# Modulation columns in tiles and on a DMA queue of their own, and the scratch of the expert selection in the free end of a ring buffer

## The chip, the core and the metric

The kernel runs on one core of one Trainium2 chip. The metric is the device time of the whole kernel in microseconds (us). A core has five engines that run beside each other and wait for one another through semaphores: TensorE (PE: matrix products; PEld are its weight loads), VectorE (DVE), ScalarE (ACT), GpSimd (POOL) and SyncE (SP), which here only issues transfers from HBM.

## The reference

Two layers work on 256 tokens of width 1024. Each layer has a token mixer (layer 0 a gated short convolution, layer 1 differential attention) and then a PEER block; each of these four sub-layers is modulated by `shift`, `scale` and `gate` and closed by a layer norm:

```
m = silu(c) @ ada_w + ada_b ;  shift, scale, gate = split(m, 3)
h = x * (1 + scale) + shift
x = layer_norm(ALPHA * x + (1 + gate) * f(h)) * ln_g + ln_b
```

PEER scores 2 x 128 keys for each of 8 heads, takes the best 16 on either side, the best 16 of their pairs (g, the softmax of those), and then sums `g * gelu(h . u[idx]) * v[idx]` over the chosen experts. There are 128 x 128 experts, and u and v are 16384 x 1024 each.

## The kernel before

PEER is computed densely: for all experts, with a gate matrix that is zero where an expert is not chosen. The 128 blocks of 128 experts are taken in three parts, `CHUNKS = (0, 46, 88, 128)`. A *U step* (24 products of 256 columns) forms the activations of a block, which go through gelu into `ring`, a buffer of 88 blocks. A *G step* forms the gates of eight tokens for all blocks of a part (one-hot matrices A and B on VectorE, 16 small products on TensorE) and multiplies them into the ring (line 840). A *V step* (12 products of 512 columns, line 874) adds a block's part to the output in four accumulators. The order is: U of part 0 beside the selection of the experts; U of part 1 with G of part 0; V of part 0 mixed with U of part 2 and G of part 1; V of the rest of parts 0 and 1 with G of part 2; then V of part 2 alone, 40 steps, called the last third of V here (it is 480 of 1536 products). The place between the last G step and V of part 2 is called the junction: V of part 2 can't start before every gate of part 2 is in the ring.

Every matrix weight comes as a 128 x 1024 tile (512 KB) into a pool `raw` and is split in two: ScalarE copies the high part (`spt<-raw`, line 87), VectorE subtracts it to get the low part (`spt<-raw,spt`, line 90). The V steps split their activations in the same way (`wh`, `wl`), once for two steps. TensorE multiplies high by high, high by low and low by high. `raw` has STREAM = 6 tiles (12 more in the convolution, 4 more in attention), `spt` has SPBUFS = 10. `pipeline(steps, 3)` starts the loads and splits of a step three steps before its products.

The modulation is computed by columns on VectorE: a column is 128 outputs of `silu(c) @ ada_w`, one 512 KB load and one multiply-and-sum of 128 x 1024 (line 177); eight make a unit, and a short addition puts a unit into `mod`. There are 96 columns. Those of the first sub-layer and some more are done in the convolution; 48 are spread over the PEER block of layer 0 and eight over that of layer 1, by a generator `fill` that `steps` advances: two columns a call, issued on SP's queue into the same `raw` tiles as the weights:

```
w = raw()
sync.dma_start(w, ada_w[i, s, part, n])
return lambda: dve.scalar_tensor_tensor(w, w, 1.0, csb, op0=ALU.mult, op1=ALU.mult, accum_out=dst)
```

`late` (`Norm.affine`, line 297) multiplies X by ln_g and adds ln_b of the norm before, from two more `raw` tiles; `prep` (line 196) transposes the gate into rows.

The program fixes what each engine computes, but a scheduler of the framework sets the order on each engine, from its own estimate of the times. `behind(name)` and `issue_after` tell it that an instruction must not be put ahead of a named one; an instruction on an engine waits in that order, so that one which waits holds up all behind it on its engine.

Of the kernel before, what the change touches and what calls it, by code (L numbers as in the profile page):

```python
# [11 lines left out]
F32 = mybir.dt.float32  # L12
F32R = mybir.dt.float32r
F16 = mybir.dt.float16
# [22 lines left out]
CHUNKS = (0, 46, 88, 128)  # L37
SPBUFS = 10
STREAM = 6
RING = CHUNKS[2]  # L40
# [3 lines left out]
def tile_trunk(ctx: ExitStack, tc: tile.TileContext, x, c, columns, ada_w, ln_g, ln_b, conv_w_in_a, conv_w_in_b,  # L44
# [134 lines left out]
    def ada_unit(i, s, part):  # L179
# [7 lines left out]
        yield  # L187

    def mod_rows(i, s, part, pool):

        t = pool.tile([P, D], F32, tag="a", name="rows")
        for hf in range(2):
            ps = bank()
            for q in range(4):
                n = 8 * part + 4 * hf + q
                pe.transpose(ps[:, q * P:(q + 1) * P], mod[:, 2 * i + s, n:n + 1].to_broadcast([P, P]), ident)
            copy(t[:, hf * 512:(hf + 1) * 512], ps)
        return t
# [18 lines left out]

    def ln_params(i, s):
        gb = raw(), raw()
        sync.dma_start(gb[0], rows_bcast(ln_g[i, s], D))  # L220
        sync.dma_start(gb[1], rows_bcast(ln_b[i, s], D))
        return gb
# [12 lines left out]
    class Norm:  # L235
# [55 lines left out]

        def affine(self, _):

            gb = ln_params(self.i, self.s)
            for t in range(NT):
                for n, op in enumerate((ALU.mult, ALU.add)):
                    dve.tensor_tensor(X[:, t, :], X[:, t, :], gb[n], op=op)

    def abank():
# [157 lines left out]
    def attn_mixer(j, li, hT, ap, prep, late):  # L457
# [145 lines left out]
        def steps():  # L603
# [10 lines left out]
            for h0 in range(0, HEADS, 2):  # L614
                n = 0
                for q in (h0 // 2, 4 + h0 // 2):
                    for st in [project_step(attn_w_qk[j, m], m, hT, use, abank, SUBS[m % 2]) for m in (2 * q, 2 * q + 1)]:
                        if h0 >= 2 and n >= 2:
                            yield (lambda h1=h0 - 2, t=n - 2: weights(h1, t), lambda a, h1=h0 - 2, t=n - 2: values(h1, t, a))
                        yield st  # L620
                        n += 1
                w = []
                if h0 == last:
                    yield None, lambda _: w.extend(weights(last, t) for t in range(NT))
                q = h0 // 2
                yield (lambda q=q: v_first(q), lambda a, q=q: v_second(q, a))
                if h0 >= 2:
                    yield None, lambda _, h1=h0 - 2: norm(h1, 1)
                if h0 == 4:
                    yield None, late  # L630
            yield None, prep
# [14 lines left out]
    def peer(i, hT, pp, fill, prep, late):  # L646
# [63 lines left out]
        ab = scratch(128).bitcast(F16).rearrange("p (n h k) -> p n h k", n=2, h=PH)  # L710

        def topk(t):
            sv, si = svs[t], sis[t]
# [3 lines left out]

            cand = sp.tile([P, PH, NCAND], F32, tag="sp", name="cand")
            dve.tensor_tensor(cand[:, :, 0:16], s0[:, :, 0:1].to_broadcast([P, PH, 16]), s1, op=ALU.add)
# [20 lines left out]

            f = sp.tile([P, 6, P], F32, tag="sp", name="f")
            pos = po.rearrange("t h k -> t (h k)")
# [21 lines left out]
            for n in range(2):  # L764
                eq = sp.tile(shape, F16, tag="sp", name="eq")
                dve.tensor_tensor(eq, ab[:, n, :, None, :].to_broadcast(shape),
                                  iota_a[:, None, :, :].to_broadcast(shape), op=ALU.is_equal)
                keys = sp.tile(shape, F16, tag="sp", name="keys")
                copy(keys, sif4[:, :, n, :, None].to_broadcast(shape))
# [39 lines left out]
        def G_step(c, tg):  # L809
# [22 lines left out]
            def second(ab):  # L832
# [6 lines left out]
                r = ring[:, s:s + n, ts8]  # L839
                dve.scalar_tensor_tensor(r, ps.rearrange("p t j -> p j t"), 1.0 / GSCALE, r, op0=ALU.mult, op1=ALU.mult)  # L840

# [4 lines left out]
        def V_steps(jp, engs):  # L846
            st = {}

            def first(jj):
                if jj == 0:  # L850
# [6 lines left out]
                    if jp == KEYS // 2 - 4:  # L857
                        act.activation(junk, st["w"][0][:, 0, 0:1].bitcast(F32), AF.Sqrt, bias=eps, scale=0.0)
                    sub(dve, st["w"][1], w, st["w"][0].bitcast(F32))
                st[jj] = load(peer_v[i, (2 * jp + jj) * KEYS:(2 * jp + jj + 1) * KEYS, :], engs[jj])  # L860
# [25 lines left out]
        def steps():  # L886
# [29 lines left out]
            for n, (gs, u) in enumerate(zip(gates(1, n2), us(2))):  # L916
                yield next(v01)
                yield u
                yield from gs
                if n % 2 == 1:  # L920
                    yield advance(fill)
            gs = gates(2, n0 + n1 - n2 - 5)
            for n, v in enumerate(v01):
                if n:
                    yield from next(gs, ())
                yield v
            for n, v in enumerate(vs(2)):
                yield v
                if n % 3 == 2:
                    yield advance(fill)  # L930
                if n == 6:
                    yield None, late
                if n == n2 - 8:
                    yield drain(fill)
                    yield None, prep

        pipeline(steps(), 3)
# [15 lines left out]
    ordered.clear()  # L953
    fill = units((0, 1, 2), (1, 0, 0), (1, 0, 1), (1, 0, 2), (1, 1, 0), (1, 1, 1))
    with tc.tile_pool(name="pp", bufs=1) as pp:
# [9 lines left out]
    with tc.tile_pool(name="pp", bufs=1) as pp:  # L965
        late, norm = norm.affine, Norm(1, 1, None, ada)
        acc = peer(1, hT, pp, units((1, 1, 2)), norm.prepare, late)
    norm(acc)
# [48 lines left out]
```

## Time and profile before

| | |
|---|---|
| time, median of 3 runs | 1957.65 us (1955.34 to 1959.71) |
| profiled execution: its own time, its span | 1956.54 us, 1954.8 us |
| PE busy | 1885.1 us, 96% |
| PEld, DVE, ACT, POOL busy | 88%, 79%, 46%, 0% |
| granted TensorE clock, mean | 0.988 |
| read from HBM | 375.42 MB, 193 GB/s over the span |

The page is of one execution. "PE busy" counts products that overlap, so what a stretch costs is read from the starts of products and from the gaps between them. In the rows, `out<-in` are the program's tiles with numbers left out, `[1.20 <-DVE wl L90]` says that the engine had been idle for 1.20 us and what ended that, and "L177" is a line of the kernel before. The changed kernel has other line numbers: 177 is 196 there for the columns in question, 297 is 323, 372 is 399, 840 is 870, 874 is 905.

### The profile page before, as it was taken

To read this page: it belongs to the slowest core of one execution; us is meant where nothing else is said; L and a number is where in the kernel's file an instruction comes from. 1 tells how busy PE (TensorE), PEld (TensorE's weight loads), DVE (VectorE), ACT (ScalarE), POOL (GpSimd) and SP (SyncE) were. 2 spreads that over 40 slices of the span, in tenths; PEclk is the share of its full clock that TensorE was granted. 3 is DMA by queue.
4 is the path that set the end of the run, shared out by engine and by line. 5 is a ranking of instruction groups with operands and counts; after the bars stand their busy time and mean duration, and the time that the engine had idled before them with its cause. 6 is when DMAs were issued, how large, how long until landed. Compare 5 with 4: busy or idle time off the path is not lost.

```text
span 1954.8 us, 36946 instructions
## 1 busy us (share of the span) xinstructions
PE 1885.1 (96%) x14858; PEld 1720.6 (88%) x14858; DVE 1550.6 (79%) x3138; ACT 905.3 (46%) x1191; POOL 9.5 (0%) x28
## 2 busy tenths in 40 slices
PE   7969999999999999989899899999999999999897
PEld 6969999999999988867798799999999999888786
DVE  7989887887888888876677788878878766888755
ACT  4534555334444444434466545653444444444443
POOL 0000000000000000000100000000000000000000
PEclk9989999999999999999999999999999999999999
DMA  9955655556778765568753246555567555555563
GB/s 383 366 187 159 185 180 177 163 158 210 249 243 256 232 201 173 173 198 279 241 182 111 86 152 184 183 174 161 161 208 226 173 175 181 168 169 181 173 194 97
DMA packets 104412, 378.87 MB, mean 194 GB/s; under 512 B 11568, under 2 KB 12208, under 8 KB 104240
## 3 DMA queue, kind: packets, MB, share of 16 engines
q1 hardware_dynamic: 104096, 376.42, 59.8%
q8 instruction: 116, 1.90, 0.4%
q14 instruction: 56, 0.46, 0.1%
q10 hardware_dynamic: 144, 0.09, 0.0%
HBM read 375.42 MB, written 1.05 MB: 193 GB/s over the span
## 4 chain that ended last, share of the span: by engine, by line
PE 91%; DVE 5%; DMA 2%; issue 1%; ACT 1%; SPq 0%; DVEq 0%; ACTq 0%
PE acc L874 34%; PE ps L141 15%; PE ps L142 15%; PE ps L143 15%; PE ps L838 4%; DVE raw L177 2%; PE acc L352 2%; PE acc L142 2%; PE acc L141 2%; PE acc L143 2%; DVE spt L90 1%; DMA raw<-in_ada_w 1%; DMA X<-in_x 1%; PE ps L517 0%; DMA gsub<-in_attn_subln_g 0%
## 5 line engine op out<-in xcount | busy, mean ns | idle before, releaser
L87 ACT ACTIVATE spt<-raw 128x1024 fp32r<-128x1024 f32 x608 | 641.1, 1058 | 745.3 <-PE ps L142 416.5
L90 DVE TENSOR_TENSOR spt<-raw,spt 128x1024 fp32r<-128x1024 f32 x608 | 741.0, 1222 | 171.3 <-ACT spt L87 166.5
L141 PE MATMUL ps<-hh,spt 128*128 128x256 f32 x2400 | 684.9, 286 | 2.9 <-DVE hh L214 2.4
L142 PE MATMUL ps<-hl,spt 128*128 128x256 f32 x2400 | 681.0, 284 | 0.6 <-DVE hl L90 0.6
L143 PE MATMUL ps<-hh,spt 128*128 128x256 f32 x2400 | 680.5, 284 | 0.0
L874 PE MATMUL acc<-spt,wh 128*128 128x512 f32 x2048 | 565.9, 396 | 4.4 <-ACT wh L87 4.4
L141 PEld LDWEIGHTS ps<-hh,spt 128*128 128x128 f32 x2400 | 460.6, 192 | 6.8 <-issue 3.0
L142 PEld LDWEIGHTS ps<-hl,spt 128*128 128x128 f32 x2400 | 461.4, 192 | 4.0 <-DVE hl L90 0.9
L143 PEld LDWEIGHTS ps<-hh,spt 128*128 128x128 f32 x2400 | 461.3, 192 | 0.0
L874 PEld LDWEIGHTS acc<-spt,wh 128*128 128x128 f32 x2048 | 375.9, 188 | 75.8 <-ACT wh L87 4.6
L874 PE MATMUL acc<-spt,wl 128*128 128x512 f32 x1024 | 319.6, 392 | 3.6 <-DVE wl L90 3.6
L874 PEld LDWEIGHTS acc<-spt,wl 128*128 128x128 f32 x1024 | 191.9, 188 | 44.8 <-DVE wl L90 5.1
L177 DVE SCALAR_TENSOR_TENSOR raw<-raw,csb 128x1024 f32<-128x1024 f32 x96 | 116.1, 1223 | 57.8 <-DMA raw<-in_ada_w 57.7
L87 ACT ACTIVATE wh<-ring 128x512 fp32r<-128x512 f32 x128 | 79.9, 627 | 159.0 <-PE acc L874 148.9
L840 DVE SCALAR_TENSOR_TENSOR ring<-ps,ring 128x368 f32<-128x368 f32 (+2 forms) x192 | 98.1, 512 | 68.6 <-PE ps L838 68.0
L825 DVE TENSOR_TENSOR A<-iota_e,jT 128x1024 f16<-128x1024 f16 x192 | 131.0, 683 | 0.0
L829 DVE TENSOR_TENSOR B<-B,gT 128x368 f16<-128x368 f16 (+2 forms) x384 | 125.1, 334 | 4.0
L90 DVE TENSOR_TENSOR wl<-ring,wh 128x512 fp32r<-128x512 f32 x128 | 88.0, 689 | 38.7 <-ACT wh L87 38.2
L838 PEld LDWEIGHTS <-A 128*128 128x128 f16 x3072 | 91.0, 96 | 31.1 <-issue 14.3
L838 PE MATMUL ps<-B,A 128*128 128x46 f16 (+2 forms) x3072 | 111.7, 182 | 6.6 <-DVE B L829 6.6
L805 ACT ACTIVATE ring<-ps 128x512 f32<-128x512 f32 x128 | 74.7, 584 | 33.8 <-PE ps L143 33.7
L827 DVE TENSOR_TENSOR B<-iota_e,iT 128x368 f16<-128x368 f16 (+2 forms) x192 | 63.4, 331 | 0.0
(204 smaller groups left out, 1179.9 us busy)
## 6 DMA issues: line engine op xcount, KB each, us to landing
raw<-in_peer_u SPq DMA_DIRECT2D x256, 512.0 KB, 3.8
raw<-in_peer_v SPq DMA_DIRECT2D x256, 512.0 KB, 3.9
raw<-in_ada_w SPq DMA_DIRECT2D x96, 512.0 KB, 4.7
raw<-in_peer_w_q SPq DMA_DIRECT2D x32, 512.0 KB, 4.1
raw<-in_attn_w_qk SPq DMA_DIRECT2D x16, 512.0 KB, 4.4
raw<-in_conv_w_in_a SPq DMA_DIRECT2D x12, 512.0 KB, 10.2
raw<-in_conv_w_in_b SPq DMA_DIRECT2D x12, 512.0 KB, 10.2
raw<-in_conv_w_out SPq DMA_DIRECT2D x8, 512.0 KB, 7.2
```

The costliest lines, as they stand in the source:

```text
L87: act.activation(o, i, AF.Copy, scale=scale)
L90: return eng.tensor_tensor(o, a, b, op=ALU.subtract)
L141: pe.matmul(ps, ah, bh, start=first, stop=False)
L142: pe.matmul(ps, ah, bl, start=False, stop=False)
L143: pe.matmul(ps, al, bh, start=False, stop=last)
L177: return lambda: dve.scalar_tensor_tensor(w, w, 1.0, csb, op0=ALU.mult, op1=ALU.mult, accum_out=dst)
L805: act.activation(ring[:, s:s + 2, :].rearrange("p j t -> p (j t)"), st["ps"], AF.Gelu)
L825: dve.tensor_tensor(by_two(A), numbers(0, KEYS), pairs(jT, KEYS), op=ALU.is_equal)
L829: dve.tensor_tensor(by_two(B[:, h]), by_two(B[:, 1]), pairs(gT[:, h], n), op=ALU.mult)
L838: pe.matmul(ps[:, t, :], A[:, t, :], B[:, h, t, :], start=h == 0, stop=h == 1)
L840: dve.scalar_tensor_tensor(r, ps.rearrange("p t j -> p j t"), 1.0 / GSCALE, r, op0=ALU.mult, op1=ALU.mult)
L874: pe.matmul(acc[t][hf], lhs[:, jj, rows], rhs[:, hf * 512:(hf + 1) * 512], start=first and jp == 0 and jj == 0, stop=last and last_pair an ...
```

## The change

Four things change. The 56 columns of the two PEER blocks go into two tiles of their own (`side`), loaded from GpSimd's queue, and one column is computed a call instead of two, while the next is being loaded; in the places where `fill` is advanced, the column is put behind `last["mark"]`, the last multiplication of a G step or the last `wl` of a V step. The calls come at other places (two of three steps; the last third of V takes 22 columns instead of 12). `late` becomes a generator; in PEER it loads into `side` tiles from GpSimd's queue and is moved from the junction to the last ten V steps. The scratch of the selection (`cand`, `f`, `eq`, `keys`) moves from the `spt` tiles to the unused end of the ring, two buffers each for `eq` and `keys`, one of `f` for each half of the tokens. For the space, STREAM goes from 6 to 5 and SPBUFS from 10 to 9, for the whole kernel.

```
-SPBUFS = 10
-STREAM = 6
+SPBUFS = 9
+STREAM = 5
...
+    def side():
+        return stream.tile([P, D], F32, tag="side", name="side", bufs=2)
+
+    def single_columns(*which):
+        def compute(at, a, n, w):
+            dve.scalar_tensor_tensor(w, w, 1.0, csb, op0=ALU.mult, op1=ALU.mult, accum_out=a[:, n:n + 1])
+            if n == KC - 1:
+                dve.tensor_tensor(mod[at], a, ada_bT[at], op=ALU.add)
+        loaded = None
+        for i, s, part in which:
+            a = small.tile([P, KC], F32, tag="ada", name="ada", bufs=2)
+            at = slice(None), 2 * i + s, slice(KC * part, KC * part + KC)
+            for n in range(KC):
+                w = side()
+                pool.dma_start(w, ada_w[i, s, part, n])
+                if loaded:
+                    compute(*loaded)
+                    yield
+                loaded = at, a, n, w
+        compute(*loaded)
+        yield
...
-        def affine(self, _):
-            gb = ln_params(self.i, self.s)
+        def affine(self, *tiles):
+            gb = ln_params(self.i, self.s, *tiles)
+            yield
             for t in range(NT):
                 for n, op in enumerate((ALU.mult, ALU.add)):
                     dve.tensor_tensor(X[:, t, :], X[:, t, :], gb[n], op=op)
+                yield
...
+        cand = scratch(PH * NCAND).rearrange("p (h k) -> p h k", **hk)
+        fs = [scratch(6 * P).rearrange("p (n k) -> p n k", n=6) for _ in range(NT)]
+        eqs, keyss = ([scratch(1024).bitcast(F16).rearrange("p (h k a) -> p h k a", h=PH, k=TOPK) for _ in range(2)]
+                      for _ in range(2))
...
-            cand = sp.tile([P, PH, NCAND], F32, tag="sp", name="cand")
-            f = sp.tile([P, 6, P], F32, tag="sp", name="f")
+            f = fs[t]
-                eq = sp.tile(shape, F16, tag="sp", name="eq")
+                eq, keys = eqs[n], keyss[n]
-                keys = sp.tile(shape, F16, tag="sp", name="keys")
...
-                if n % 2 == 1:
-                    yield advance(fill)
+                if n % 3 != 0:
+                    yield advance(fill, 1, ("mark",))
...
+            rest = late(side, pool)
             for n, v in enumerate(vs(2)):
                 yield v
-                if n % 3 == 2:
-                    yield advance(fill)
-                if n == 6:
-                    yield None, late
+                if n % 3 != 0 and n < n2 - 10:
+                    yield advance(fill, 1, ("mark",))
+                if n == n2 - 10:
+                    yield drain(fill)
+                    yield advance(rest)
                 if n == n2 - 8:
-                    yield drain(fill)
                     yield None, prep
+                if n in (n2 - 7, n2 - 5):
+                    yield advance(rest, 1, ("mark",))
...
-    fill = units((0, 1, 2), (1, 0, 0), (1, 0, 1), (1, 0, 2), (1, 1, 0), (1, 1, 1))
+    fill = single_columns((0, 1, 2), (1, 0, 0), (1, 0, 1), (1, 0, 2), (1, 1, 0), (1, 1, 1))
...
-        acc = peer(1, hT, pp, units((1, 1, 2)), norm.prepare, late)
+        acc = peer(1, hT, pp, single_columns((1, 1, 2)), norm.prepare, late)
```

What stands where on an engine, before and now, is shown at three places. On VectorE, at the junction of layer 0, `L825`, `L827`, `L829` (now 855, 857, 859) build the A and B of a G step, `L840` (870) multiplies its gates into the ring, `L177` is a column and `L297` the affine step. Before:

```order
L840 SCALAR_TENSOR_TENSOR ring<-ps,ring 128x40x8
L825 TENSOR_TENSOR A<-iota_e,jT 128x1024
L827 TENSOR_TENSOR B<-iota_e,iT 128x320
L829 TENSOR_TENSOR B<-B,gT 128x320
L90 TENSOR_TENSOR spt<-raw,spt 128x1024
L829 TENSOR_TENSOR B<-B,gT 128x320 x2
L177 SCALAR_TENSOR_TENSOR raw,ada<-raw,csb 128x1024
...
L840 SCALAR_TENSOR_TENSOR ring<-ps,ring 128x40x8 x2
L90 TENSOR_TENSOR wl<-ring,wh 128x512 x2
L297 TENSOR_TENSOR X<-X,raw 128x1024 x2
```

Two columns stand there in all, with one more L829 between them; those two rows repeat the ones shown and are left out. Now, at the same place:

```order
L870 SCALAR_TENSOR_TENSOR ring<-ps,ring 128x40x8
L855 TENSOR_TENSOR A<-iota_e,jT 128x1024
L857 TENSOR_TENSOR B<-iota_e,iT 128x320
L859 TENSOR_TENSOR B<-B,gT 128x320 x4
L870 SCALAR_TENSOR_TENSOR ring<-ps,ring 128x40x8 x2
L90 TENSOR_TENSOR wl<-ring,wh 128x512 x2
L90 TENSOR_TENSOR spt<-raw,spt 128x1024 x2
L90 TENSOR_TENSOR wl<-ring,wh 128x512
L196 SCALAR_TENSOR_TENSOR side,ada<-side,csb 128x1024 x2
```

The columns, the affine step and one low part of a weight have left the junction; the first columns stand behind the third `wl`. In layer 1 the same has become of the low part and the affine step; no column stood there.

On GpSimd, from the start of the program on; `z` are tiles of the convolution, `dist` is attention's. Before:

```order
masks.py:199 AFFINE_SELECT ident<-ident 128x128
L163 IOTA iota_a 128x256
L372 MEMSET z 128x2 x8
L478 IOTA dist 128x256
L479 AFFINE_SELECT dist<-dist 128x256
```

And now:

```order
L163 IOTA iota_a 128x256
L399 MEMSET z 128x2 x2
L206 DMA side<-in_ada_w 128x1024 x2
L399 MEMSET z 128x2 x6
L206 DMA side<-in_ada_w 128x1024 x46
L245 DMA side<-in_ln_g 128x1024
```

The loads of the first two columns of the PEER block stand ahead of the third `z` and wait for nothing, so they are issued as soon as GpSimd comes to them; the other 46 of layer 0 follow behind the last `z`, each waiting for a free `side` tile.

On VectorE, at the first layer norm (behind the convolution), where the line numbers are 25 higher now: `L268` adds X and the mixer's output, `L273` and `L277` are its mean and the reciprocal of its deviation, `L286` writes a normalised half of X. Before:

```order
L268 SCALAR_TENSOR_TENSOR spt,mv<-X,spt 128x1024
L90 TENSOR_TENSOR spt<-raw,spt 128x1024
L90 TENSOR_TENSOR kl<-kr,kh 128x256
L273 TENSOR_SCALAR mv<-mv 128x1
L277 RECIPROCAL mv<-mv 128x1
L256 TENSOR_TENSOR gbc<-smT,mod 128x8
L286 TENSOR_SCALAR X<-spt,mv 128x1024
L258 TENSOR_TENSOR gbc<-gbc,mod 128x8
```

The reciprocal and the write of the second half stand behind these rows. And now:

```order
L90 TENSOR_TENSOR spt<-raw,spt 128x1024
L293 SCALAR_TENSOR_TENSOR spt,mv<-X,spt 128x1024 x2
L90 TENSOR_TENSOR kl<-kr,kh 128x256
L298 TENSOR_SCALAR mv<-mv 128x1 x2
L281 TENSOR_TENSOR gbc<-smT,mod 128x8
L283 TENSOR_TENSOR gbc<-gbc,mod 128x8
L302 RECIPROCAL mv<-mv 128x1 x2
L311 TENSOR_SCALAR X<-spt,mv 128x1024 x2
```

Both reciprocals, the second of which needs the sum over the second half, now stand ahead of both writes.

## Rows read from the trace of the kernel before

**Rows 1.** Page: share of the span in the chain that ended last.
```profile
PE 91%; DVE 5%; DMA 2%; issue 1%; ACT 1%; SPq 0%; DVEq 0%; ACTq 0%
```

**Rows 2.** Windows: length, busy us (xcount), clock, DMA share, GB/s.
```profile
10.00:80.00 70.00, 63.51 (x505) 61.79 (x506) 61.64 (x95) 36.84 (x58) 0.40 (x4) 1.00 1.03 408
...
858.00:972.00 114.00, 110.80 (x478) 90.73 (x479) 75.42 (x95) 50.77 (x59) 7.44 (x10) 0.99 0.74 250
```

**Rows 3.** Timeline (start, duration), layer 0, junction: TensorE and VectorE.
```profile
847.81 0.61 PE L874 MATMUL acc<-spt,wl 128*128 128x512 f32 x2
...
853.62 1.23 DVE L177 SCALAR_TENSOR_TENSOR raw<-raw,csb 128x1024 f32<-128x1024 f32 x1 [0.64 <-DMA raw<-in_ada_w]
...
856.03 1.23 DVE L177 SCALAR_TENSOR_TENSOR raw<-raw,csb 128x1024 f32<-128x1024 f32 x1 [0.93 <-DMA raw<-in_ada_w]
...
858.84 1.54 PE L874 MATMUL acc<-spt,wh 128*128 128x512 f32 x4 [3.03 <-ACT wh L87]
```

**Rows 4.** Timeline, layer 1, the same junction.
```profile
1826.83 0.61 PE L874 MATMUL acc<-spt,wl 128*128 128x512 f32 x2
...
1828.58 1.22 DVE L90 TENSOR_TENSOR spt<-raw,spt 128x1024 fp32r<-128x1024 f32 x1
...
1829.71 0.79 DVE L829 TENSOR_TENSOR B<-B,gT 128x320 f16<-128x320 f16 x3
...
1833.27 2.11 PE L874 MATMUL acc<-spt,wh 128*128 128x512 f32 x8 [1.32 <-ACT wh L87]
...
1833.55 2.36 DVE L297 TENSOR_TENSOR X<-X,raw 128x1024 f32<-128x1024 f32 x2 [1.06 <-DMA raw<-in_ln_g]
...
1836.57 1.20 PE L874 MATMUL acc<-spt,wl 128*128 128x512 f32 x4 [1.20 <-DVE wl L90]
```

**Rows 5.** Timeline, TensorE: last product of the V stage, layers 0 and 1.
```profile
972.25 0.39 PE L874 MATMUL acc<-spt,wl 128*128 128x512 f32 x1
...
1943.49 0.39 PE L874 MATMUL acc<-spt,wl 128*128 128x512 f32 x1
```

**Rows 6.** Timeline, layer 0, last third of V: a late column.
```profile
919.91 1.23 DVE L177 SCALAR_TENSOR_TENSOR raw<-raw,csb 128x1024 f32<-128x1024 f32 x1 [2.50 <-DMA raw<-in_ada_w]
...
922.68 0.69 DVE L90 TENSOR_TENSOR wl<-ring,wh 128x512 fp32r<-128x512 f32 x1
...
923.42 0.74 PE L874 MATMUL acc<-spt,wl 128*128 128x512 f32 x2 [1.35 <-DVE wl L90]
```

**Rows 7.** Waits, last third of V, layer 0: us in total, times, longest.
```profile
DVE raw L177 <- DMA raw<-in_ada_w: 18.9, 8, 3.5
```

**Rows 8.** DMA issues: xcount, KB, median us to landing; 858:945, then 0:125.
```profile
raw<-in_ada_w SPq DMA_DIRECT2D x12, 512.0 KB, 5.1
...
raw<-in_ada_w SPq DMA_DIRECT2D x40, 512.0 KB, 8.7
...
raw<-in_conv_w_in_a SPq DMA_DIRECT2D x12, 512.0 KB, 10.2
```

**Rows 9.** Start: timeline of GpSimd, and a piece of the chain.
```profile
1.94 0.13 POOL L372 MEMSET z<- 128x2 f32 x2
...
3.23 10.03 DMA X<-in_x
```

**Rows 10.** Timeline, first layer norm: VectorE, ScalarE, TensorE.
```profile
126.05 1.15 ACT L270 ACTIVATE hl<-spt,mv 128x1024 fp32r<-128x1024 f32 x1 [0.71 <-DVE spt L268]
...
126.67 0.82 DVE L286 TENSOR_SCALAR X<-spt,mv 128x1024 f32<-128x1024 f32 x1
...
127.55 1.76 PE L207 MATMUL ps<-ident,X 128*128 128x128 f32 x7 [13.49 <-DVE X L286]
...
127.85 0.81 DVE L286 TENSOR_SCALAR X<-spt,mv 128x1024 f32<-128x1024 f32 x1
```

**Rows 11.** Waits, whole span: ScalarE for a free weight buffer.
```profile
ACT spt L87 <- PE ps L142: 416.5, 225, 5.7
...
ACT spt L87 <- PE acc L874: 230.9, 161, 2.8
```

More of the change, by code (lines that the diff above doesn't have):

```diff
@@ L216, in make_hT, with ln_params @@
         return hh, hl
[L218 to L221, printed above, removed]
+    def ln_params(i, s, tile=raw, queue=sync):
+        gb = tile(), tile()
+        queue.dma_start(gb[0], rows_bcast(ln_g[i, s], D))
+        queue.dma_start(gb[1], rows_bcast(ln_b[i, s], D))
         return gb
@@ L629, in steps @@
                 if h0 == 4:
-                    yield None, late
+                    yield drain(late())
             yield None, prep
@@ L839, in second @@
                 r = ring[:, s:s + n, ts8]
-                dve.scalar_tensor_tensor(r, ps.rearrange("p t j -> p j t"), 1.0 / GSCALE, r, op0=ALU.mult, op1=ALU.mult)
+                last["mark"] = dve.scalar_tensor_tensor(r, ps.rearrange("p t j -> p j t"), 1.0 / GSCALE, r, op0=ALU.mult,
+                                                        op1=ALU.mult)
             return first, second, True
@@ L858, in first @@
                         act.activation(junk, st["w"][0][:, 0, 0:1].bitcast(F32), AF.Sqrt, bias=eps, scale=0.0)
-                    sub(dve, st["w"][1], w, st["w"][0].bitcast(F32))
+                    last["mark"] = sub(dve, st["w"][1], w, st["w"][0].bitcast(F32))
                 st[jj] = load(peer_v[i, (2 * jp + jj) * KEYS:(2 * jp + jj + 1) * KEYS, :], engs[jj])
@@ L926, in steps @@
                 yield v
+            rest = late(side, pool)
             for n, v in enumerate(vs(2)):
                 yield v
-                if n % 3 == 2:
-                    yield advance(fill)
-                if n == 6:
-                    yield None, late
+                if n % 3 != 0 and n < n2 - 10:
[3 more added lines that the diff above has]
+                    yield advance(rest)
                 if n == n2 - 8:
-                    yield drain(fill)
                     yield None, prep
+                if n in (n2 - 7, n2 - 5):
+                    yield advance(rest, 1, ("mark",))
         pipeline(steps(), 3)
```

## The prediction

> **What bounds the kernel now.** I read the shares of the chain that ended last first: TensorE holds 91% of it [rows 1], so a microsecond counts only where TensorE stops or starts later. Then the waits over the whole span. ScalarE waits 416.5 and 230.9 us in all for a free `spt` tile [rows 11]: the split weights stand ready and wait for TensorE, which goes at its own pace in nearly every stage. So there are only a few places to win or lose anything: the start, the layer norms, and the junctions. For these I read timelines.
>
> The junction and V of part 2 are the place where layer 0 and layer 1 differ. From the last product before the junction to the last product of V it is 972.25 - 847.81 = 124.44 us in layer 0 and 1943.49 - 1826.83 = 116.66 us in layer 1 [rows 3 to 5]. The work of TensorE is the same 480 products. Layer 0 has columns on VectorE there, layer 1 has none. In layer 0's junction, two columns stop VectorE until their load lands (0.64 and 0.93 us) and take 1.23 us each, ahead of the multiplications for which the first V product waits until 858.84 [rows 3]. Later a column waits 2.50 us for its load; the `wl` behind it on VectorE ends at 923.37 and the next product starts at 923.42, after 1.35 us of idle TensorE [rows 6]. Over the stage the columns wait 18.9 us, 8 times [rows 7]. VectorE is busy 75.42 of 114 us, so it is the order and not the amount that makes it late; DMA stands at 0.74 and 250 GB/s, against 408 GB/s at a share of 1.03 in the start [rows 2].
>
> **Part 1: columns and affine step off the junctions (gain).** The new order puts the columns of layer 0 behind the third `wl`, the affine step near the end of V, and one low part of a weight behind the first two `wl`. Layer 1 shows what is left, since it has no columns: 1833.27 - 1826.83 = 6.44 us of junction [rows 4]. In it the low part stands between the multiplications by gT and holds them from 1828.58 to 1829.71, 1.13 us [rows 4]. Without it: 5.31 us. V itself takes 1943.49 - 1833.27 = 110.22 us [rows 4, 5]; of this 1.20 us is a wait for the second `wl`, which stands behind the affine step (2.36 us and a wait of 1.06) [rows 4]. Without it: 109.02 us. Together 114.33 us, which I take for both layers. Layer 0 gains 124.44 - 114.33 = 10.1 us, layer 1 gains 2.3 us: 12.4 us. If only layer 1's present stage is reached in layer 0 and nothing in layer 1, it is 7.8 us; that is the lower bound while the columns are in time.
>
> Whether 22 columns instead of 12 fit into V: ten more at 1.23 us add 12.3 us to VectorE's 75.42, some 88 of 109 us. In DMA, 5.2 MB more in 109 us add 48 GB/s to 250, about 300, below the 408 that the start reaches [rows 2]. Whether each load is in time: there are two tiles, a load can start when the column two calls earlier is done, and two calls lie three steps apart (3 x 12 x 0.227 = 8.2 us, the 0.227 being 109.02 us over 480 products). Less the column itself, 7.0 us are left for a load. In this stage the present loads of the same size take 5.1 us, the median of 12 [rows 8]. So they are in time, by 1.9 us, if GpSimd's queue is as fast as SP's; no GpSimd load stands in the trace of before. The affine step now falls among the last ten steps, four instructions of half of 2.36 us, covered by products for which all weights stand ready. Behind the affine loads on GpSimd stand the ten instructions that it now has in this stretch, 7.44 us in all [rows 2]; they make attention's bias, which is wanted only after the next norm, so I cost that wait at 0.
>
> The Trainium skill, DMA: Bandwidth & Descriptors, section "Anatomy of one DMA — SWDGE (gpsimd) path", gives for a transfer issued there about 2.0 us and its bytes over 436 GB/s; a 512 KB load would by this take 3.2 us, an estimate from that page, and be in time as well. No row here shows one.
>
> **Part 2: the first two column loads go to the start (loss).** GpSimd has nothing to wait for ahead of them, and gets to them behind its `z` at 1.94 us [rows 9]. There DMA is at its limit, 408 GB/s from 10 to 80 us [rows 2], and X's load (3.23 us, 10.03 long) is itself a link of the chain [rows 9]. 2 x 524 KB = 1.05 MB at 408 GB/s is 2.57 us. Since loads set the pace up to the first layer norm, I carry 2.6 us to the end. The bounds are 0 (they displace only loads that are early) and 2.6. A separate queue would help if it had its own bandwidth, but the share of 1.03 is of all the engines the core has.
>
> The same page of the Trainium skill, section "Issuing engines are not separate DMA queues", says so directly: loads started by any engine run on the same 16 DMA engines and interleave. The trace of before can't show that for GpSimd, but it speaks against any gain from the separate queue as such, and for counting the collision in full.
>
> **Part 3: order at the first norm (loss).** Both reciprocals now stand ahead of both writes of X. The second needs ScalarE's square of the second half, 126.05 + 1.15 = 127.20 [rows 10]. The first write started at 126.67, so it starts later by over half a microsecond; the second started at 127.85 and can start only behind the first, 0.82 later, some 0.7 us late [rows 10]. TensorE has by then been idle since the products before, and begins at 127.55 with transposes of X [rows 10]. I add another 0.7 us since the last low part of the output projection stands behind more columns on VectorE: half of one instruction of 1.22 us [rows 4], as I do not know how it will fall. Sum 1.5 us, bounds 0 and 3.
>
> **Part 4: smaller pools and moved scratch (nothing).** A tile less of 6 and of 10 costs lead, and lead is what the kernel has: the 648 us of waiting for free `spt` tiles say that ScalarE is ahead and blocked [rows 11]. I cost it at 0. If that cover were gone, the place would be a stage which consumes weights at the highest rate, the eight steps of the output projections, one split of a weight each (1.22 us on VectorE, [rows 4]): up to 9.8 us. The scratch frees the `spt` tiles that selection held, in a stage in which TensorE goes at pace: 0, and no more than the 2.3 us which one junction gains could be found there.
>
> **Sum.** -12.4 + 2.6 + 1.5 = -8.3 us. The profiled execution took 1956.54 us in the end, so 1948.2 us; the median of the three runs lies 1.1 us above the profiled one, so the forecast is 1949.0 us, rounded by 0.3.
>
> **Rivals.** *Slower: the column loads are late.* If a load on GpSimd's queue takes T above 7.0 us, each column waits, and with it every `wl` behind the mark. Two tiles give a column every (T + 1.15)/2; the twenty columns in the thirty steps up to the last ten then take 10 us longer for each us of T over 7.0. Since the `wl` are made three steps ahead, some 7 us of it (8.2 less a column) are absorbed. At T = 10.2, the median of twelve loads in the start [rows 8], it costs 32 - 7 = 25 us: 1949 + 25 = 1974 us. The gain of 8.3 us is used up at T = 8.5, and from 8.9 on the kernel is measurably slower. For it: the 8.7 us which the same columns take in the saturated start [rows 8], and that no load from GpSimd is known here. Against it: 5.1 us in this stage, and 300 of 408 GB/s.
>
> *No change: the stage gains half.* A column that is only sometimes late costs what the one at 919.91 cost, 1.35 us [rows 6]; four of them in layer 0 and a junction which keeps 1 us leave some 6 of the 12.4 us, against 4.1 us lost (5.6 at the upper bounds): 1955 to 1957 us. Or the pools bite in half the output steps, which gives 1949 + 5 = 1954 us.
>
> *Faster by more: the start doesn't pay.* If the two early loads fill gaps in front of X, and the norm's order costs nothing because TensorE waits for the other half anyway, 4.1 us come back: 1945 us.
>
> **How the numbers follow.** About 0.2%, 3.9 us, is what a measurement of this kernel can tell from no change; faster then means below 1953.7 us and slower above 1961.6. The forecast, with its own range of 1946 to 1952, has 0.5; more than that (1945) 0.17; no change 0.2; late columns 0.13. Of the "no change" cases some 0.04 still count as faster; of late columns, some 0.02 stop short of the bound. That is 0.71 faster, 0.18 same (0.2 - 0.04 + 0.02), 0.11 slower. The range of 1943.5 to 1958 leaves out most of the slower case and a bit on the other end.
>
> **What would show it.** Right: in both layers some 114 us from the last V product before the junction to the last one of V, the first product of V about 5.3 us behind; columns in V with no waits for loads, at landings of under 7 us on GpSimd's queue; X's load longer by about 2.6 us, and the first transposes of X later by about 4 us in all. Wrong: waits of columns for `side` in V and of products for `wl` behind them; ScalarE's waits for free `spt` gone and TensorE's waits for weights in their place, which would mean that the pools were not spare; a start that has not moved.

## The result: slower, and the profile after

The changed kernel takes 1971.85 us (median of 4 runs, 1969.61 to 1975.97), the one before 1958.02: a ratio of 1.0071 (95% interval 1.0056 to 1.0086). I had forecast 1949.0, faster. Its profiled span is 1967.8 us, 13.0 longer than before.

Both kernels run the same 14858 products on TensorE. I set each product of one profiled execution beside the same product of the other (same tile, same turn), and read how much later it starts, the lag. It stays constant while TensorE goes at its own pace, and changes only where one kernel stalls:

| stretch | predicted, us | changed - before, us |
|---|---|---|
| start to past the first layer norm | +4.1 | +2.2 |
| layer 0, selection | 0 | +1.8 |
| layer 0, gates of part 0 beside U | 0 | +1.3 |
| layer 0, junction and V of part 2 | -10.1 | -6.7 |
| norm behind it | 0 | +3.2 |
| attention | 0 | +6.4 |
| layer 1, selection; gates beside U | 0; 0 | +1.8; +1.3 |
| layer 1, junction and V of part 2 | -2.3 | +2.3 |
| last norm and the end | 0 | -0.6 |

The lines of the changed kernel's timeline that answer to [rows 3 to 5], the two junctions and the ends of V (start, duration, engine, line, operation; in brackets the idle time before it and what ended it):

```profile
852.16 0.61 PE L905 MATMUL acc<-spt,wl 128*128 128x512 f32 x2
...
859.90 2.50 PE L905 MATMUL acc<-spt,wh 128*128 128x512 f32 x5 [1.25 <-ACT wh L87]
...
970.92 0.39 PE L905 MATMUL acc<-spt,wl 128*128 128x512 f32 x1
...
1837.48 1.23 DVE L90 TENSOR_TENSOR spt<-raw,spt 128x1024 fp32r<-128x1024 f32 x1 [1.65 <-PE acc L905]
...
1841.47 0.45 PE L868 MATMUL ps<-B,A 128*128 128x40 f16 x2 [2.87 <-DVE B L859]
...
1845.95 1.65 PE L905 MATMUL acc<-spt,wh 128*128 128x512 f32 x3 [1.24 <-ACT wh L87]
...
1957.11 0.39 PE L905 MATMUL acc<-spt,wl 128*128 128x512 f32 x1
```

From last product to last product this is 118.76 us in layer 0 (124.44 before) and, from 1837.22, 119.89 in layer 1 (116.66 before). The table's changes are some 0.9 us lower, because 30 small products of the last G step (0.92 us) now stand behind the last V product before the junction and no longer ahead of it. In layer 1 VectorE waits 1.65 us for TensorE to release a tile, with a low part of a weight that stands ahead of the gates; no such wait is in [rows 4]. TensorE then idles 2.87 us in one piece, where it idled 1.27 and 1.18 before (layer 1 of the kernel before):

```profile
1828.72 0.19 PE L838 MATMUL ps<-B,A 128*128 128x40 f16 x1 [1.27 <-DVE B L829]
...
1830.09 0.19 PE L838 MATMUL ps<-B,A 128*128 128x40 f16 x1 [1.18 <-DVE B L829]
```

In layer 0 the changed kernel has the same wait and the same idle piece.

Behind that idle time the granted clock is low. Windows of the changed kernel (length, busy time of PE, PEld, DVE, ACT, POOL, then the clock, DMA share and GB/s), first layer 0, then layer 1:

```profile
859.90:863.00 3.10, 3.10 (x7) 2.47 (x8) 1.27 (x2) 0.46 (x1) 0.00 (x0) 0.50 0.00 0
...
1846.00:1849.00 3.00, 3.00 (x7) 2.42 (x8) 1.22 (x2) 0.41 (x1) 0.00 (x0) 0.50 0.02 5
```

0.50 is the 1.2 GHz level. The first 24 products of V take 7.85 us there (859.90 to 867.75); at the full clock, in the run affine_in_mix below, 5.57. From its first to its last product V takes 111.0 us in layer 0 and 111.2 in layer 1 here, 108.7 in both layers of affine_in_mix: so the low clock behind the junction costs some 2.4 us in each layer.

What answers to [rows 11] is the reading that I got most wrong. Waits of the changed kernel over its whole span (total us, times, longest):

```profile
ACT spt L87 <- PE acc L905: 211.6, 123, 2.6
ACT spt L87 <- PE ps L143: 180.3, 108, 2.2
...
DVE spt L90 <- issue: 126.2, 123, 2.9
DVE spt L90 <- PE ps L142: 113.2, 118, 2.0
DVE spt L90 <- PE acc L905: 64.1, 44, 2.8
```

ScalarE waits less for free tiles, and VectorE now waits for them itself, 113.2 + 64.1 us ("issue" is a wait for which the profile shows no cause). The kernel before has

```profile
DVE spt L90 <- ACT spt L87: 166.5, 187, 5.6
...
DVE spt L90 <- PE ps L142: 1.2, 2, 0.6
```

There VectorE waited for ScalarE's high part (3.9 us in the changed kernel) and hardly ever for a tile; so not all of its new waiting is added time. The rows that answer to [rows 8, 9] are as forecast: GpSimd's loads land in time, and X lands later.

```profile
3.25 12.59 DMA X<-in_x
```

```profile
side<-in_ada_w POOLq DMA_DIRECT2D x56, 512.0 KB, 5.0
```

### The profile page after: what moved, and what is told of

It is laid out like the page before. It is cut to its first block, busy times and chain, and to the rows that moved or that the text cites. A ratio compares the mean times of both kernels' runs of the same rounds, so it can differ in the third digit from the quotient of the medians.

```text
span 1967.8 us, 37106 instructions
## 1 busy us (share of the span) xinstructions
PE 1891.9 (96%) x14858; PEld 1726.2 (88%) x14858; DVE 1548.1 (79%) x3138; ACT 905.7 (46%) x1191; POOL 44.0 (2%) x88
## 4 chain that ended last, share of the span: by engine, by line
PE 69%; issue 22%; DVE 5%; DMA 2%; ACT 1%; POOL 1%; SPq 0%; DVEq 0%; POOLq 0%; ACTq 0%
PE acc L905 19%; PE ps L141 13%; PE ps L142 13%; PE ps L143 13%; PE ps L868 3%; PE acc L142 2%; PE acc L141 2%; DVE raw L177 2%; PE acc L143 1%; DVE spt L90 1%; POOL side L206 1%; PE acc L379 1%; DMA X<-in_x 1%; PE ps L544 0%; DMA side<-in_ln_b 0%
## 5 line engine op out<-in xcount | busy, mean ns | idle before, releaser
L868 PE MATMUL ps<-B,A 128*128 128x46 f16 (+2 forms) x3072 | 116.3, 182 | 5.8 <-DVE B L859 5.7
L868 PEld LDWEIGHTS <-A 128*128 128x128 f16 x3072 | 93.0, 96 | 30.5 <-issue 13.2
L196 DVE SCALAR_TENSOR_TENSOR side<-side,csb 128x1024 f32<-128x1024 f32 x56 | 67.9, 1219 | 10.7 <-DMA side<-in_ada_w 10.7
## 6 DMA issues: line engine op xcount, KB each, us to landing
raw<-in_conv_w_in_a SPq DMA_DIRECT2D x12, 512.0 KB, 10.5
```

Of the source, the lines that this page charges most:

```text
L868: pe.matmul(ps[:, t, :], A[:, t, :], B[:, h, t, :], start=h == 0, stop=h == 1)
```

## Experiments

Each has its median time and its ratio to the kernel before, executed beside it (1958.3 to 1958.6 us in all of them), with the 95% interval. What a stretch loses is read from one profiled execution of each, as in the table. Theory P is that the smaller pools cost the time, Q that the side loads and the moved affine step do. The first four take the change apart.

**pools_only**
```
-SPBUFS = 10, STREAM = 6
+SPBUFS = 9, STREAM = 5
```


> The kernel before with nothing changed but STREAM 6 to 5 and SPBUFS 10 to 9. Theory P (the smaller pools cost the time, because fewer tiles change the order on TensorE and VectorE in attention and shorten the lead elsewhere): 8 to 12 us slower than before, with some 6 us of it between the first norm after the PEER block of layer 0 and the end of attention (980 to 1120 us), 1 us in each layer while part 0's gates run beside U. Theory Q (the loss is of the side loads and the moved affine step, the pools were spare as I had predicted): within 1 us of before.

1967.86 us, ratio 1.0047 (1.0031 to 1.0064). 10.7 us are lost in attention and 1.3 in each layer's gates beside U. P holds.

**order_only**
```
 (the changed kernel's calls and marks; pools and scratch as before)
+w = raw(); sync.dma_start(w, ada_w[i, s, part, n])
+rest = late()
```


> Pools of 10 and 6 and the scratch in the weight buffers as before; columns one by one behind the marks and the affine step in two pieces near the end of V, but in the ring's own raw tiles and from SyncE's queue. Theory P: 6 to 10 us faster than before, all of it between the junction and the end of V of part 2 in layer 0 (124.4 us before), since nothing else is touched; attention as before. Theory Q: no more than 3 us faster, because the norm behind V of part 2 starts 3 us later, as in the changed kernel.

1948.90 us, 0.9945 (0.9929 to 0.9962). Junction and V of layer 0 gain 9.0 us, layer 1's 1.5 (P had expected nothing there); the norm behind V does lose 3.0. P's size, with Q's loss inside it.

**side_on_sync**
```
-pool.dma_start(w, ada_w[i, s, part, n])
+sync.dma_start(w, ada_w[i, s, part, n])
...
-rest = late(side, pool)
+rest = late(side)
```


> The changed kernel with the loads of the side tiles issued from SyncE's queue and no longer from GpSimd's. Theory P: X lands as before (first transposes at 13.3 us and not at 15.9), so 2 to 3 us faster than the changed kernel, still 9 to 12 us slower than before, with the loss in attention unchanged. Theory Q: 6 us or more faster than the changed kernel, since the start and the norm behind PEER both come back.

1964.19 us, 1.0028 (1.0019 to 1.0038). X lands as before (lag 0.3 us), but SyncE issues the same two loads from 17.4 us on and the lag is 3.7 us at 36 and 3.0 past the norm. So the two loads cost about as much wherever they stand in the start. Attention keeps its loss (5.6), as P said; but the kernel is 7.7 us faster than the changed one, which is Q's size, and the norm behind PEER loses 0.9 us in place of 3.2, which is half of Q's reason. Neither theory holds whole, and the profile shows only 3.5 of the 7.7 us (span 1964.3); the rest stays open.

**scratch_only**
```
-f = sp.tile([P, 6, P], F32, tag="sp", name="f")
+f = fs[t]          # cand, eq, keys likewise, in the ring's free end
```


> The kernel before with the selection's scratch moved to the free end of the ring, nothing else. If the 1.8 us that each layer loses at about 262 and 1240 us (TensorE waits 1.55 us for the transposed scratch) come from the scratch: 3.6 us slower than before, 1.8 in each layer. If they come from the smaller pools: within 0.5 us of before.

1964.11 us, 1.0026 (1.0016 to 1.0036). Not free: 5.8 us slower than before, which neither side had expected: 1.1 us in each selection, and 4.3 in the junction and V of layer 1. There the affine step, whose code was not touched, has come ahead of the gates on VectorE and waits for its load:

```profile
1835.32 2.36 DVE L297 TENSOR_TENSOR X<-X,raw 128x1024 f32<-128x1024 f32 x2 [3.06 <-DMA raw<-in_ln_g]
...
1839.26 3.67 PE L877 MATMUL acc<-spt,wh 128*128 128x512 f32 x8 [4.94 <-ACT wh L87]
```

The next runs ask which pool it is, and where the norm's 3 us go.

**spt_9**, **spt_8**, **stream_5**: the kernel before with one number changed.
```
 SPBUFS = 9    |    SPBUFS = 8    |    STREAM = 5
```


> The kernel before with SPBUFS 9, and STREAM left at 6. Theory odd (each load takes two tiles, a high and a low; with nine, one of them is always left over, so that VectorE, which works in order, waits with a low part for TensorE to free a tile, where with ten only ScalarE waited): nearly all of the 9.6 us which both smaller pools cost, 8 to 11 us slower than before, and waits of VectorE for free spt tiles of over 100 us in all where there are none before. Theory raw (the stream of five is what shortens the lead): within 2 us of before.

1973.28 us, 1.0074 (1.0057 to 1.0091): 14.7 us slower than before, more than the 8 to 11 of the odd-number theory and more than both smaller pools together (9.6). Attention loses 14.2. Why it is more there with STREAM 6 than with 5 stays open.

> The kernel before with SPBUFS 8, one tile fewer still. Theory odd: four whole pairs; VectorE waits for free tiles under 20 us in all, and the time is within 4 us of before, less than with nine. Theory size (what counts is the number of tiles): slower than with nine, by 10 us or more against before.

1969.40 us, 1.0052 (1.0035 to 1.0069).

> The kernel before with STREAM 5, and SPBUFS left at 10. Theory odd: within 2 us of before. Theory raw: 8 to 11 us slower than before.

1956.58 us, 0.9990 (0.9981 to 1.0000). The stream of raw tiles was spare, as predicted; the weight tiles were not. The waits, first with nine tiles, then with eight:

```profile
DVE spt L90 <- issue: 129.3, 121, 2.9
DVE spt L90 <- PE ps L142: 61.5, 78, 4.9
DVE spt L90 <- PE acc L874: 51.3, 35, 2.3
```

```profile
ACT spt L87 <- PE ps L142: 434.6, 232, 5.6
...
DVE spt L90 <- PE ps L142: 1.7, 2, 0.9
```

With eight, VectorE's waits are gone: that half of the odd-number theory holds. Its time doesn't follow: eight tiles are 10.8 us slower than before, 3.9 less than nine, and not within the 4 us that I had expected. They lose 7.1 us in attention, and some 3 at the first norm and 1 in each selection and beside each layer's gates. So the odd tile explains who waits, and the number itself costs too; that expectation of mine fell.

**affine_early**
```
-if n == n2 - 10: ...; yield advance(rest)
+if n == 9: yield advance(rest)
-if n in (n2 - 7, n2 - 5):
+if n in (12, 15):
```


> As order_only, but the affine step's loads are issued in step 9 of V of part 2 and its two pieces put behind the marks of steps 12 and 15, away from the last wl. If the 3 us which order_only loses at the norm behind V come from the affine step delaying the last wl (and with it the release of the PEER tiles, in whose place the load lamr goes that VectorE then waits for): that norm as before, 945 to 947 us... in all 1944.5 to 1947.5 us, 2 to 3 us faster than order_only. If the columns themselves delay it, or the order of the loads: within 1 us of order_only's 1948.9.

1949.29 us, 0.9953 (0.9936 to 0.9970): no better than order_only. The norm loses only 0.8 us now, but junction and V gain 5.7 in place of 9.0. Some 2.3 us of this are lost in V near 905 us, where the affine step now stands between the columns on VectorE. Another 1.2 are lost in the junction, with the idle pieces of order_only (1.27 and 1.18 us) but a granted clock of 0.51 from 852 to 855.5 us. The norm's cause was right; the cure was wrong.

**changed_10_4**, **changed_attention_10**, **changed_old_scratch**, **affine_in_mix**: parts undone in the changed kernel, and the affine step elsewhere.
```
+SPBUFS = 10, STREAM = 4                        # changed_10_4
+(tenth[0] if tenth and turn[0] == 9 else sp)   # changed_attention_10, in spt()
+f = sp.tile(...)   # cand, eq, keys likewise    changed_old_scratch
+if n in (3, 6, 9): yield advance(rest, 1, ("mark",))   # affine_in_mix, in the loop of U of part 2
```


> The changed kernel with SPBUFS 10 again, paid for with STREAM 4 in place of 5 (the tiles take the same space). If the ninth-tile theory holds: attention (7.6 us), and the gates beside U (2.2 us in layer 0, 2.3 in layer 1) come back, about 12 us faster than the changed kernel, some 1960 us, with VectorE's waits for free spt tiles gone. If the side tiles and their queue are the main cost: within 3 us of the changed kernel's 1971.9.

1958.60 us, 0.9991 (0.9981 to 1.0001): 13 us come back, 9.9 in the profiles. Attention and the gates lag by 0.1 and 0.0 us more than before, and VectorE's waits for free tiles are gone.

> The changed kernel, with a tenth spt tile in attention alone (from attention's own space). If the loss in attention comes from the order that nine tiles give on TensorE there (scores of the next heads behind more products of the output projection, then 6 us of idle TensorE at the transposes of the softmax): only that comes back, 6.5 to 8.5 us faster than the changed kernel, 1963 to 1966 us, and no wait over 2 us at those transposes. If it comes from anything carried in from the stages before: within 2 us of the changed kernel.

1962.37 us, 1.0013 (1.0002 to 1.0024), 9.5 faster, more than expected. In the profile the lag changes by -2.9 in attention, where the changed kernel's changes by +6.4; but the norm ahead of it loses 6.8 in place of 3.2, so that the two together give back 5.7. So not only attention has changed. TensorE's waits in that stretch (1056 to 1100 us):

```profile
PE ps L580 <- ACT aT L89: 1.7, 2, 1.2
```

The changed kernel's TensorE in the same place, with the scores (k,q) behind the output projection (yh, yl), and then out of work:

```profile
1065.94 1.09 PE L379 MATMUL acc<-spt,yh 128*128 128x512 f32 x4
...
1070.33 0.70 PE L544 MATMUL ps<-k,q 64*128 64x256 f32 x2
...
1080.87 1.09 PE L568 MATMUL ps<-ident,s 128*128 128x128 f32 x4 [5.75 <-DVE s L566]
```

VectorE waits there for those scores, and not for a weight tile, and behind the idle piece the granted clock is at its lower level:

```profile
1072.94 0.69 DVE L548 TENSOR_TENSOR s<-ps,bias 128x512 f32<-128x512 f32 x1 [4.89 <-PE ps L544]
...
1080.00:1086.00 6.00, 4.44 (x22) 3.80 (x23) 1.68 (x7) 1.22 (x5) 0.00 (x0) 0.50 0.20 74
```

The kernel with eight tiles (spt_8) has the same order, and TensorE idles 4.68 us there:

```profile
1082.87 1.00 PE L541 MATMUL ps<-ident,s 128*128 128x128 f32 x4 [4.68 <-DVE s L539]
```

The kernel before has the scores first, and a granted clock of 1.00 from 1080 to 1086 us:

```profile
1062.23 0.70 PE L517 MATMUL ps<-k,q 64*128 64x256 f32 x2
...
1066.32 1.09 PE L352 MATMUL acc<-spt,yh 128*128 128x512 f32 x4
...
1072.35 0.60 PE L541 MATMUL ps<-ident,s 128*128 128x128 f32 x4
```

> The changed kernel with the selection's scratch back in spt tiles. If the 1.8 us at the transposes of the selection in each layer come from the scratch: 3.6 us faster than the changed kernel, and if its junction in layer 1 (2.3 us longer than before) does too, as the run with the scratch alone suggests (4.3 us longer), 6 us faster: 1966 to 1968 us. If they come from the nine tiles: within 1 us of the changed kernel.

1964.62 us, 1.0034 (1.0023 to 1.0045), 7.2 faster (3.8 in the profiles): selection 0.0 in both layers, the junction and V of layer 1 at -0.3 where the changed kernel has +2.3. In the changed kernel TensorE waits in the selection for VectorE with the transposes:

```profile
263.98 0.30 PE L807 MATMUL ps<-ident,ring 128*128 128x128 f32 x1 [1.55 <-DVE ring L804]
```

The junction of layer 1 doesn't show what the scratch costs. With the old scratch TensorE idles there as in the changed kernel, but the granted clock behind it is 1.00, and V takes 108.7 us:

```profile
1840.15 0.43 PE L866 MATMUL ps<-B,A 128*128 128x40 f16 x2 [2.87 <-DVE B L857]
...
1844.60:1847.60 3.00, 3.00 (x13) 2.46 (x14) 2.12 (x3) 0.39 (x1) 0.00 (x0) 1.00 0.02 5
```

> As order_only (pools and scratch of before, single columns in raw tiles), with the affine step moved into the stage in which U of part 2, G and V are mixed (VectorE busy 53.6 of 70 us there, DMA at 0.73) in place of the last ten V steps. If the norm behind V of part 2 lost its 3 us in order_only to the affine step beside the last wl: norm as before, 945 to 947 us. If the columns keep it late anyway: within 1 us of order_only's 1948.9.

1945.70 us, 0.9932 (0.9916 to 0.9949): the fastest, 12.7 us under the kernel before. Its TensorE, layer 0:

```profile
848.08 0.61 PE L903 MATMUL acc<-spt,wl 128*128 128x512 f32 x2
...
854.52 1.65 PE L903 MATMUL acc<-spt,wh 128*128 128x512 f32 x6 [1.32 <-ACT wh L87]
...
963.22 0.39 PE L903 MATMUL acc<-spt,wl 128*128 128x512 f32 x1
```

That is 115.14 us against my 114.33, and 115.18 in layer 1. The norm behind V is 0.5 us earlier than before.

The last four ask about the start and about whose the gain is.

**changed_held**, **rest_undone**, **rest_undone_held**, **affine_only**
```
+if held: held.pop(); dve.memset(w[:, 0:1], 0.0)   # the two _held, ahead of the load, which waits for it;
                                                   # each column comes one call later
+SPBUFS = 10, STREAM = 4, old scratch, affine step as in affine_in_mix   # the two rest_undone
+if n in (3, 6, 9): yield advance(rest, 1, ("mark",))   # affine_only, in the kernel before
```


> The changed kernel; VectorE writes one element of each of the first two side tiles (0.1 us) behind the mark of the first call, so that GpSimd's first two loads wait for it and leave the start. If those two loads are the 2.6 us which X lands later: the first transposes of X at 13.3 us as in the kernel before, and 2 to 4 us faster than the changed kernel. If the start pays for something else: within 1 us of it at the end, or X as late as in the changed kernel.

1973.60 us, 1.0066 (1.0050 to 1.0083). X's transposes start at 13.14 us, so X's delay is explained; but the total isn't better, for attention, still with nine tiles, now loses 13.2 us, with TensorE idle in the same place for 5.8 us. Why it loses twice as much as in the changed kernel stays open.

> Side tiles and GpSimd's queue for the columns as in the changed kernel; SPBUFS 10 and STREAM 4, the old scratch, and the affine step in the mix from raw tiles. If nothing but the two early loads is left of the loss: affine_in_mix and 2.6 us, that is 1947.5 to 1949.5 us. If GpSimd's queue or the two tiles make columns late: 1951 us or more, with waits of columns for side tiles of over 10 us in all.

1951.51 us, 0.9963 (0.9949 to 0.9977), between the two. Columns wait 14.3 us in all for side tiles, but the lag of 5.0 us comes in the start, and 7.5 are gained in junction and V of layer 0.

> As rest_undone, with the first two loads held back as in changed_held. If the queue itself is neither gain nor loss: 1944.5 to 1947 us, as affine_in_mix. If a queue of its own is worth something: under 1944 us.

1946.31 us, 0.9932 (0.9916 to 0.9949), as affine_in_mix. Held back, the loads give back 5.2 us, twice their 2.6. With them held, the queue of its own is neither gain nor loss.

> The kernel before with only its affine step moved into the mix (raw tiles, SyncE's queue); columns in pairs and in their old places. If the columns in the junction and in V of part 2 of layer 0 are what costs, as I predicted: 1.5 us in layer 1 and 1 to 2 in layer 0, 1954.5 to 1956.5 us. If the affine step alone made V of layer 0 late: 1949 us or less.

1953.33 us, 0.9973 (0.9964 to 0.9983). The affine step is worth 5.2 us, rather more than the 2 to 4 expected (its profile shows 2.9); the columns, by difference to affine_in_mix, the other 7.6.

## Why the prediction was wrong

The step that failed is part 4: "A tile less of 6 and of 10 costs lead, and lead is what the kernel has ... I cost it at 0." I read ScalarE's 647 us of waiting as a reserve. A full ring does show that weights are early on average; it doesn't show what one tile fewer does to the engine next in line, or to the order that the scheduler makes. A load takes two tiles, a high and a low. With nine, VectorE is often left with a low part and no tile; it works in order, and gates and splits stand behind it, as in the junction. But these waits aren't what most of the time is lost by: with eight tiles they are gone, and 10.8 us are lost all the same.

The largest loss lies in attention. With nine tiles as with eight, TensorE has the scores behind the output projection there; VectorE waits for the scores, TensorE then idles in one piece, and in the changed kernel the clock behind it is low. That the number of tiles is the cause is shown by changed_10_4, which gives 13 us back, and by spt_9 beside stream_5. changed_attention_10 gives back the idle piece, but its time is not attention's alone. How the number of tiles leads the scheduler to that order is not shown. My bound, 9.8 us, came from the output projections; the convolution's lost nothing, attention lost its time at the scores, and spt_9 is beyond the bound, at 14.7. The sign that I had named, TensorE waiting for weights, did not come either.

"The scratch ...: 0" failed too: 3.6 us in the two selections. What was bounded at 2.3 us of gain had no bound on the side of loss. That the scratch is the cause is shown by undoing it; but with ten tiles it costs 2.2 us there (scratch_only, changed_10_4), so that the nine tiles have a part in it. In the junction and V of layer 1, scratch_only loses 4.3 us, with the affine step ahead of the gates. The changed kernel's 2.3 us there are something else: the low clock behind the junction costs as much, and the order is the same with the old scratch. That the scratch acts through the scheduler's order (with nothing waiting for the scratch itself) fits the rows of scratch_only, but is argued.

Part 1 was right in its mechanism: order_only and affine_in_mix gain 10.5 and 10.8 us in the two stretches where I had 12.4. Two terms in it were mis-sized. "Without it: 5.31 us" of junction: 6.44 in affine_in_mix, since there the low part stays between the multiplications by gT. And the changed kernel has 7.74 and 8.73 (0.92 of it the 30 products that came over from ahead of it), with one idle piece of 2.87 us and the half clock behind it, of which the sum had nothing. V itself, put at 109.02, takes 108.7 in affine_in_mix. The affine step "covered by products" was wrong: VectorE's last wl came later, and with it the load of attention's parameters, for which VectorE then waits ahead of the norm (changed kernel):

```profile
970.10 0.42 DVE L494 TENSOR_TENSOR lp<-lamr 128x128 f32<-128x128 f32 x1 [1.63 <-DMA lamr<-in_attn_lambda]
...
978.74 3.80 PE L232 MATMUL ps<-ident,X 128*128 128x128 f32 x16 [7.42 <-DVE mv L298]
```

From V's end to these transposes it is 7.82 us; in the kernel before, from 972.25, 4.70:

```profile
976.95 3.80 PE L207 MATMUL ps<-ident,X 128*128 128x128 f32 x16 [4.31 <-DVE mv L273]
```

In affine_in_mix, with the affine step elsewhere and the columns where order_only has them, the norm is as early as before.

Part 2 was right for X: 2.58 us at its first transposes (13.30 to 15.88), against 2.57 worked out. To carry it unchanged to the end was not: past the first norm the lag is 2.2 us in the changed kernel and 5.0 in rest_undone. The Trainium skill, DMA: Bandwidth & Descriptors, section "Issuing engines are not separate DMA queues", says that loads issued by different engines run on the same 16 DMA engines and interleave. side_on_sync agrees: the two loads cost 2.5 us ahead of the norm from SyncE's queue and 2.65 from GpSimd's. The 3.2 us for such a load, the prediction's estimate from the section "Anatomy of one DMA — SWDGE (gpsimd) path" of that page of the Trainium skill, is near the shortest seen, 3.5; the median was 5.0. Part 3 was too high: of 1.5 us, 1.2 show at the norm, and all of it is gone 20 us later.

The rival on the slower side, late columns, did not happen: 10.7 us of waits in all, 6 of them, none over 2.9 us. The slower kernel came by a way that I had put at 0, and at 5 us in a rival.

## What to carry to other kernels

A producer that waits for free buffers does not prove that a buffer is spare: ask who takes the last one, and whether an engine with other work queued behind it will have to wait in its place. Where two tiles are taken at a time, an odd number changes who waits; it doesn't say what the number costs, so time the even one too. Where a scheduler orders the engines from its own estimates, compare the whole order for every pool or scratch that changes, above all where dependent work is interleaved closely, as in attention.

## What the runs showed that I had not expected

The two early loads cost 2.6 us at X and up to 5.0 past the first norm. After an idle piece of 2.87 us the clock stood at 0.50 for the next 3 us in both layers of the changed kernel, but in changed_old_scratch at 0.50 in layer 0 and at 1.00 in layer 1. After pieces of 1.27 and 1.18 us it stayed at 1.00 in affine_in_mix, but fell in changed_10_4. So rows of idle time alone do not settle it, and a difference of 2 to 3 us behind a junction can be the clock's and not the change's.

Over the whole span the mean granted clock is 0.983 in the changed kernel and 0.988 before. By these figures TensorE stands some 20 us longer at the lower level, an estimate (twice 1.7% of 1967.8 us, less twice 1.2% of 1954.8). Part of the 13.0 us is therefore the clock's, and not idle time itself.
